# Moving S5 work and weight splits in a fp32 decoder trunk, and cutting its last product into 384 and 128 positions

## The chip, the cores and the metric

The kernel runs on one core of a Trainium2 chip. The metric is the device time of one execution in microseconds. The core has TensorE (PE in the profile: matmuls; PEld: its weight loads), VectorE (DVE), ScalarE (ACT), GpSimd (POOL), SyncE (SP), and 16 DMA engines that move data between memory and the core's SBUF. PSUM banks (`ps`) take the results of matmuls.

## The reference

Two decoder layers on 512 positions of width 1024, in fp32. Each has a mixer (an S5 diagonal state space model beside retention), attention to a memory, and a SwiGLU FFN of inner width 2816, all with RMS norms ahead and residual sums behind; a last RMS norm ends it.

```
for l in range(DEPTH):                       # 2
    proj = rms_norm(x, norm_mix[l]) @ w_in[l]
    u, q, k, v, g = split(proj)
    y_ssm = rms_norm(s5_mixer(u, ...), s5_out_norm[l])
    y_ret = retention(q, k, v, g, ...)
    x = x + concatenate([y_ssm, y_ret]) @ w_out[l]
    x = x + memory_cross_attention(rms_norm(x, ...), ...)
    h = rms_norm(x, norm_ffn[l])
    x = x + (silu(h @ w_gate[l]) * (h @ w_up[l])) @ w_down[l]
return rms_norm(x, norm_final)
```

## The kernel before

Activations lie transposed, 128 features on the partitions and the 512 positions along a row: `xs[0..7]` are eight tiles `x` of 128x512.

**Products.** A fp32 product is made of three fp32r matmuls (`mm3`): high part by high part, high by low, low by high. Activations are split in two tiles (`u_acth` and `u_actl` in the FFN: ACT writes the high part, DVE the difference), and so is each weight chunk of 128x1024.

**Weights.** `prep_chunk` (line 479) brings a chunk: SP issues the load of `raw`, ACT copies it to the high part `w`, and DVE subtracts, `w<-raw,w`, for the low part. For some chunks of layer 0 (`ADDED`) the low part is made without DVE: ACT writes minus the rounded raw tile into it, and POOL issues a DMA that adds the chunk from memory to it. This is called an adding load below; it reads the chunk a second time. There are five `raw` slots.

**FFN** (line 1524). The 22 blocks of 128 inner features go in four parts per layer, 0-6, 6-12, 12-18, 18-22 (`FPARTS`, line 32). In each part the products of gate and up run first, in pairs with 256-column matmuls whose results DVE and ACT merge in `u_gs` and `u_us`; these end in the activations `acts`. Then the part's down product runs: for each of eight output tiles m, six (or four) blocks of `mm3` on 512 positions, and DVE adds the result to `xs[m]`. In the last part of layer 0 the next norm is fed from each finished `xs[m]`.

**S5 work for layer 1.** The tables and matrices of layer 1's S5, in four chunks c of work, are built while layer 0's FFN runs (`s5_load`, `s5_spill`, lines 966 and 1100): DVE, ACT and POOL build, TensorE multiplies, and POOL issues DMAs to scratch memory `sp`; layer 1 fetches it later. `extra["work"]` (line 1742) says after which (first block of the part, m) a half of a chunk is taken up; each chunk has two entries.

**The last part of layer 1** is `last_down` (line 1595), which ends the program: the down product in two halves of 256 positions each; for each half eight `mm3` groups, the sum with `xs` (`u_ly`), its square (`u_lq`), sums of squares over features by TensorE with 1-column matmuls, the inverse root, its spread over the partitions by `spread`, then the output `u_fin` = `u_ly` by gain (`u_lp`) by inverse root. The first half's four outputs are made by POOL, the second's by DVE; SP sends each out.

**Order.** All engine calls are recorded as operations and a list scheduler sets the order on every engine: `due` (line 264) gives each operation a due time from TensorE's program order and the durations of a price table, and `schedule` (line 286) picks for each free engine the earliest due operation whose inputs are ready and whose slots are free. So all instructions have one line in the profile, L410.

Of the kernel before, what the change touches and what calls it, by code (L numbers as in the profile page):

```python
# [18 lines left out]
P = 128  # L19
# [13 lines left out]
HALF = SEQ // 2  # L33

# [388 lines left out]
def trunk(ctx, tc, io):  # L423
# [53 lines left out]
    held = []  # L477

    def prep_chunk(i):
        finish()  # L480
        raw = prog.buf("raw")
        Q.dma_start(out=raw, in_=io["w"][place[i]])
        hi, lo = prog.buf("w"), prog.buf("w")
        S.activation(out=hi, in_=raw, func=AF.Copy)
        if order[i][0] in ADDED and order[i][1] == 0 and (i % 2 == 0 or i > FEW):

            S.activation(out=lo, in_=raw, func=AF.Copy, scale=-1.0)
            G.dma_start(out=lo, in_=io["w"][place[i]].bitcast(F32R), accum_op=add)
        else:
            V.tensor_tensor(out=lo, in0=raw, in1=hi.bitcast(F32), op=sub)  # L490
        ready[i] = (hi, lo)
# [1032 lines left out]
    def ffn(l, nrm, nxt, extra):  # L1524
# [25 lines left out]
        for fa, fb in FPARTS[l]:  # L1550
            acts = []
# [6 lines left out]
            for f in range(fa, fb, 2):  # L1558
                gs = [gen("gs"), gen("gs")]
                us = [gen("us"), gen("us")]  # L1560

                def gated(f=f, gs=gs):
                    if f == 0:
                        nrm.root(True)
                    for g in gs:
                        V.tensor_tensor(out=g, in0=g, in1=nrm.bc, op=mul)
                        S.activation(out=g, in_=g, func=AF.Silu)
                        V.tensor_tensor(out=g, in0=g, in1=nrm.bc, op=mul)

                def merged(f=f, gs=gs, us=us):  # L1570
                    for g, u in zip(gs, us):
                        V.tensor_tensor(out=u, in0=u, in1=g, op=mul)
                    acts.extend(split(u, "act") for u in us)
                gens.append(chain("gate", f, *gs, gated))
                gens.append(chain("up", f, *us, merged))
            run_pairs(gens)
            if nxt is None and fb == NFF:
                last_down(l, fa, acts)
                return
# [15 lines left out]
    def last_down(l, fa, acts):  # L1595
# [3 lines left out]
        for half in range(2):  # L1599
            sl = slice(half * HALF, (half + 1) * HALF)  # L1600
            prog.cap = CAP if half else 2000
            acc, last, ys, ps_ = None, [], [], []

            def gains(m):
                ps_.append(gen("lp"))
                for a in range(2):
                    k = V_FIN + m - 1 + a
                    S.activation(out=ps_[-1][:, a * HALF:(a + 1) * HALF], in_=ys[m - 1 + a],
                                 func=AF.Copy, scale=vec[:, k:k + 1])

            for m in range(KT):
                ps = bank("dn")
                for f in range(n):
                    blk = m * n + f
                    b = (blk % 8) * P
                    mm3(ps[:, :HALF], cut(ws[blk // 8], slice(None), slice(b, b + P)),
                        cut(acts[f], slice(None), sl), f == 0, f == n - 1)
                y, sq = gen("ly")[:, :HALF], gen("lq")[:, :HALF]
                V.tensor_tensor(out=y, in0=ps[:, :HALF], in1=xs[m][:, sl], op=add)
                S.activation(out=sq, in_=y, func=AF.Square)  # L1620
                ys.append(y)
                if m % 2 == 1 and m < KT - 1:
                    gains(m)
                if m >= KT - 2:
                    last.append(sq)
                elif acc is None:
                    acc = sq
                else:
                    new = gen("la")[:, :HALF]
                    V.tensor_tensor(out=new, in0=acc, in1=sq, op=add)  # L1630
                    acc = new
            cols = [bank("lc")[:, :1] for _ in range(2)]
            for x in [acc] + last:
                for j in range(2):
# [3 lines left out]
            m, y, t = small("lm", 2), small("ly", 2), small("lt", 2)  # L1638
            for j in range(2):
# [8 lines left out]
            spread(pb, y, 2)  # L1648
            bc = pb[:, :HALF]
            if half == 0:  # L1650

                bc = gen("lbc")[:, :HALF]
                S.activation(out=bc, in_=pb[:, :HALF], func=AF.Copy)
            eng = G if half == 0 else V
            for i in range(KT // 2):
                y, o = ps_[i], gen("fin")
                pair = lambda x: x.rearrange("p (a t) -> p a t", a=2)
                eng.tensor_tensor(out=pair(o), in0=pair(y), op=mul,
                                  in1=bc.unsqueeze(1).to_broadcast([P, 2, HALF]))
                Q.dma_start(out=prog.perm(dest[2 * i * P:(2 * i + 2) * P, sl].rearrange(  # L1660
                    "(a p) t -> p a t", a=2)), in_=pair(o))
# [60 lines left out]
    for l in range(L):  # L1722
# [6 lines left out]
        if l + 1 < L:  # L1729
            def work(c):  # L1730
                if c == 0:
                    extra["ld"] = s5_load(l + 1)
                if c not in half:
# [3 lines left out]
            extra["work"] = {(0, 0): 0, (0, 2): 0, (6, 0): 1, (6, 2): 1, (12, 0): 2, (12, 2): 2,  # L1737
                             (12, 4): 3, (12, 6): 3}
# [103 lines left out]
```

## Time and profile before

| | us |
|---|---|
| time, median of 3 runs | 1464.76 (1464.25 to 1468.72) |
| the profiled execution | 1465.04 |
| its span | 1463.2 |
| PE busy | 1448.3 (99%) |
| DVE busy | 1185.9 (81%) |
| ACT busy | 799.3 (55%) |
| POOL busy | 101.2 (7%) |
| FFN of layer 0, parts one to three | 97.92, 95.52, 97.44 |
| FFN of layer 1, first and third part | 93.65, 92.83 |
| last down of layer 1 on PE | 24.40 |
| from there to the span's end | 10.84 |

The span is the profiled execution from first to last instruction, and the device time has 1.84 us around it. The stages are stretches of the span, cut where TensorE goes from one part's work to the next. Busy time is of the instructions that are not register, branch, semaphore or DMA-issuing ones.

### The profile page before, as it was taken

The page shows a single profiled execution, that of the slowest core. Times are in us where ns is not written, and L with a number is a line of the kernel's source. Part 1 is how long each engine was busy: PE and PEld are TensorE (multiplying, and loading weights), DVE is VectorE, ACT ScalarE, POOL GpSimd, SP SyncE. Part 2 cuts the span into 40 slices and gives each one's busy share as a digit, 9 for nine tenths or more (in the row PEclk, how much of TensorE's full clock was granted, in tenths as well). Part 3 has the DMA queues.
Part 4 walks back from the last instruction along what each step waited for, and adds up shares of the span by engine and source line. Part 5 has one row for each costly group of instructions (what it writes and reads, how often), then busy time and mean ns, then how long its engine had stood idle before and what let it go on. Part 6 is the DMA issues. An engine that isn't in the chain of part 4 may idle for free.

```text
span 1463.2 us, 23062 instructions
## 1 busy us (share of the span) xinstructions
PE 1448.3 (99%) x8784; PEld 1274.3 (87%) x8784; DVE 1185.9 (81%) x2073; ACT 799.3 (55%) x1381; POOL 101.2 (7%) x207
## 2 busy tenths in 40 slices
PE   8999999999999999999999999999999999999997
PEld 7887888888898998988988888888889989999897
DVE  8889996666999896997964989757679969869595
ACT  6798665444665463565635346644456625436264
POOL 5721000000001001002000000000000000000001
PEclk9999999999999999999999999999999999999998
DMA  8556443212135233244445444332112323413221
GB/s 286 149 121 184 158 143 128 90 58 73 58 105 177 90 131 125 98 143 155 144 139 192 141 157 137 127 133 89 62 58 73 125 77 102 144 59 125 91 87 58
DMA packets 68175, 175.35 MB, mean 120 GB/s; under 512 B 11360, under 2 KB 23008, under 8 KB 68064
## 3 DMA queue, kind: packets, MB, share of 16 engines
q1 hardware_dynamic: 64240, 160.77, 33.0%
q0 software_dynamic: 3824, 13.11, 3.5%
q8 instruction: 69, 1.13, 0.3%
q14 instruction: 42, 0.34, 0.1%
HBM read 159.43 MB, written 13.63 MB: 118 GB/s over the span
## 4 chain that ended last, share of the span: by engine, by line
PE 91%; DVE 5%; DMA 2%; ACT 1%; issue 1%; SPq 0%; DVEq 0%; ACTq 0%
PE ps L410 91%; DVE w L410 1%; DVE u_gs L410 1%; DVE u_us L410 1%; ACT w L410 1%; DMA u_angq<-in_pos_dram 0%; DMA raw<-in_w_dram 0%; DVE raw L410 0%; DMA x<-in_xT_dram 0%; DMA u_w<-in_w_dram 0%; DVE u_mt L410 0%; SPq L410 0%; DVE u_actl L410 0%; DVE u_la L410 0%; ACT u_lq L410 0%
## 5 line engine op out<-in xcount | busy, mean ns | idle before, releaser
L410 ACT ACTIVATE w<-raw 128x1024 fp32r<-128x1024 f32 x353 | 352.9, 1005 | 423.0 <-PE ps L410 347.0
L410 PE MATMUL ps<-u_nff,w 128*128 128x256 f32 x3696 | 439.2, 280 | 0.6 <-DVE w L410 0.4
L410 PEld LDWEIGHTS ps<-u_nff,w 128*128 128x128 f32 x3696 | 436.2, 188 | 4.1 <-DVE w L410 1.4
L410 DVE TENSOR_TENSOR w<-raw,w 128x1024 fp32r<-128x1024 f32 x331 | 378.8, 1151 | 51.1 <-ACT w L410 50.5
L410 PE MATMUL ps<-u_acth,w 128*128 128x512 f32 (+1 forms) x768 | 224.5, 375 | 0.3 <-ACT u_acth L410 0.3
L410 PEld LDWEIGHTS ps<-u_acth,w 128*128 128x128 f32 x768 | 139.7, 188 | 26.3 <-ACT u_acth L410 0.7
L410 PE MATMUL ps<-u_nmh,w 128*128 128x512 f32 x480 | 157.0, 398 | 0.5 <-DVE w L410 0.5
L410 PE MATMUL ps<-u_actl,w 128*128 128x512 f32 (+1 forms) x384 | 143.9, 377 | 1.4 <-DVE u_actl L410 1.2
L410 DVE TENSOR_TENSOR x<-ps,x 128x512 f32<-128x512 f32 x88 | 60.5, 689 | 99.1 <-PE ps L410 99.0
L410 PEld LDWEIGHTS ps<-u_nmh,w 128*128 128x128 f32 x480 | 89.7, 188 | 19.0 <-DVE w L410 0.9
L410 PE MATMUL ps<-u_nml,w 128*128 128x512 f32 x240 | 95.1, 396 | 0.0
L410 PEld LDWEIGHTS ps<-u_actl,w 128*128 128x128 f32 x384 | 72.2, 188 | 16.9 <-DVE u_actl L410 3.7
L410 PE MATMUL ps<-u_nch,w 128*128 128x512 f32 x256 | 81.7, 393 | 0.0
L410 PE MATMUL ps<-u_xoh,w 128*128 128x512 f32 x256 | 80.7, 392 | 0.0
L410 DVE TENSOR_TENSOR raw<-raw 128x512 f32<-128x512 f32 x88 | 60.3, 685 | 6.1 <-DMA raw<-in_ws_dram 5.9
L410 DVE TENSOR_TENSOR raw<-raw,raw 128x512 f32<-128x512 f32 x88 | 60.3, 685 | 0.3
L410 DVE TENSOR_TENSOR u_gs<-u_gs,u_nfry 128x512 f32<-128x512 f32 x88 | 59.5, 689 | 0.3
L410 POOL TENSOR_TENSOR u_fin<-u_lp,u_lbc 128x512 f32<-128x512 f32 x4 | 5.4, 1393 | 767.4 <-ACT u_lbc L410 767.4
L410 PEld LDWEIGHTS ps<-u_nch,w 128*128 128x128 f32 x256 | 48.1, 188 | 10.4
L410 PEld LDWEIGHTS ps<-u_xoh,w 128*128 128x128 f32 x256 | 48.0, 188 | 9.9
L410 PEld LDWEIGHTS ps<-u_nml,w 128*128 128x128 f32 x240 | 45.2, 188 | 9.1 <-issue 0.2
L410 PE MATMUL ps<-u_xol,w 128*128 128x512 f32 x128 | 50.3, 393 | 0.0
(369 smaller groups left out, 2463.7 us busy)
## 6 DMA issues: line engine op xcount, KB each, us to landing
raw<-in_w_dram SPq DMA_DIRECT2D x166, 512.0 KB, 3.6
raw<-in_ws_dram SPq DMA_DIRECT2D x88, 512.0 KB, 3.7
u_s5x<-sp SPq DMA_DIRECT2D x28, 256.0 KB, 4.1
w<-in_w_dram POOLq DMA_DIRECT2D x11, 512.0 KB, 5.4
u_mr<-in_memT_dram SPq DMA_DIRECT2D x12, 256.0 KB, 3.9
x<-in_xT_dram SPq DMA_DIRECT2D x8, 256.0 KB, 4.4
tu<-u_u SPq DMA_DIRECT2D x8, 256.0 KB, 3.5
u_ub<-tu SPq DMA_DIRECT2D x32, 64.0 KB, 3.5
```

The lines of the kernel that those rows point to most:

```text
L410: getattr(engines[o.eng], o.fn)(**k)
```

## The change

Three edits, which go together.

1. In layer 0's FFN the half-chunks of S5 work for layer 1 are taken up after m = 2 and m = 4 of each part's down, chunk c in part c. Before it was m = 0 and 2 for chunks 0 to 2, and m = 4 and 6 of the third part for chunk 3, which is now in the last part.
2. The down chunks 0, 2, 4 and 6, 8, 10 of layer 0's first two parts are made with adding loads: for each of six chunks, one DVE subtraction less, one ACT copy and one POOL DMA more.
3. `last_down` cuts the positions 384 and 128 instead of 256 and 256. The first piece has the `mm3` products on 384 columns; the second has one fp32 matmul in place of three products, with the raw weight (kept in `raws`) by the unsplit activation (`whole`). The first piece's outputs are eight of 128x384 each, six on POOL and two on DVE (`rest`); the second's are two of 128x512 (four row blocks of 128 positions).

```
-        if order[i][0] in ADDED and order[i][1] == 0 and (i % 2 == 0 or i > FEW):
-            S.activation(out=lo, in_=raw, func=AF.Copy, scale=-1.0)
-            G.dma_start(out=lo, in_=io["w"][place[i]].bitcast(F32R), accum_op=add)
+        if added(i):
+            add_load(lo, raw, io["w"][place[i]])

+    def added(i):
+        x = order[i]
+        if x[1] > 0:
+            return False
+        if x[0] in ADDED:
+            return i % 2 == 0 or i > FEW
+        a, b = FPARTS[0][:2]
+        if x[0] == "down":
+            return x[2] < b[1] and x[2] % 2 == 0
+        return False

+        for first in (True, False):
+            sl = slice(0, QUART) if first else slice(QUART, SEQ)
...
+                    if first:
+                        mm3(ps[:, :w], cut(ws[blk // 8], slice(None), b),
+                            cut(acts[f], slice(None), sl), f == 0, f == n - 1)
+                    else:
+                        T.matmul(out=ps[:, :w], lhsT=raws[fa + blk // 8][:, b],
+                                 rhs=whole[f][:, sl], start=f == 0, stop=f == n - 1)
...
+            for i in range(KT // per):
+                if not first:
+                    scaled(V, i)
+                elif i < KT - 2:
+                    scaled(G, i)
+                else:
+                    rest.append(lambda i=i, f=scaled: f(V, i))

-            extra["work"] = {(0, 0): 0, (0, 2): 0, (6, 0): 1, (6, 2): 1, (12, 0): 2, (12, 2): 2,
-                             (12, 4): 3, (12, 6): 3}
+            extra["work"] = {(a, m): c for c, (a, b) in enumerate(FPARTS[l]) for m in (2, 4)}
```

Where the order of instructions moves, it moves as follows. First DVE in layer 0's first part, where gate and up end and the down begins; `u_mt`, `u_mb`, `u_s5bb` are S5 rows, `u_us`, `u_actl` the FFN's. Before:

```order
L410 TENSOR_TENSOR u_us<-u_us,u_gs 128x512
L410 TENSOR_TENSOR u_mt_4667<-u_s5bb,rr_165 128x256
L410 TENSOR_TENSOR u_mb<-u_mt_4648 128x256
L410 TENSOR_TENSOR u_us<-u_us,u_gs 128x512
L410 TENSOR_TENSOR u_mb<-u_mt_4667 128x256
L410 TENSOR_TENSOR u_mt_4697<-u_s5c,pr_161 128x256
L410 TENSOR_TENSOR u_mt_4700<-u_s5c,pi_162 128x256
L410 TENSOR_TENSOR u_actl<-u_us,u_acth 128x512
L410 TENSOR_TENSOR u_mt_4697<-u_s5c,pi_162 128x256
L410 TENSOR_TENSOR u_mt_4700<-u_s5c,pr_161 128x256
L410 TENSOR_TENSOR w_110<-raw_105,w_111 128x1024
L410 TENSOR_TENSOR w_114<-raw_106,w_115 128x1024
```

The same place on DVE now:

```order
L411 TENSOR_TENSOR u_us<-u_us,u_gs 128x512
L411 TENSOR_TENSOR u_gs<-u_gs,u_nfry 128x512 x2
L411 TENSOR_TENSOR u_actl<-u_us,u_acth 128x512
L411 TENSOR_TENSOR u_us<-ps_118,u_us 128x256
L411 SCALAR_TENSOR_TENSOR u_us<-ps_122,u_us 128x512
L411 TENSOR_TENSOR u_actl<-u_us,u_acth 128x512
L411 TENSOR_TENSOR u_gs<-u_gs,u_nfry 128x512
L411 TENSOR_TENSOR u_us<-u_us,u_gs 128x512 x2
L411 TENSOR_TENSOR w_114<-raw_106,w_115 128x1024
L411 TENSOR_TENSOR u_actl<-u_us,u_acth 128x512 x2
L411 TENSOR_TENSOR u_s5bb<-u_s5b,fr_163 128x256
L411 TENSOR_TENSOR u_s5bt<-u_s5b,fi_164 128x256
```

All `u_actl` now stand ahead of the S5 rows, and one of the weight splits `w<-raw,w` is gone from between them.

Then POOL's queue in the first part, with the memsets and copies of the S5 work. Before:

```order
L410 COPY u_ckr<-u_s5c 128x4x16
L410 TENSOR_SCALAR u_cki<-u_s5c 128x4x16
L410 TENSOR_TENSOR u_diag<-s5d_139,eye_12_140 32x256
L408 MEMSET u_dt 128x512
L408 MEMSET u_car 128x512
L408 MEMSET u_cai 128x512
L410 DMA sp_181<-u_btr 128x512
```

And now:

```order
L411 COPY u_ckr<-u_s5c 128x4x16
L411 TENSOR_SCALAR u_cki<-u_s5c 128x4x16
L411 DMA w_112<-in_w_dram 128x1024
L411 TENSOR_TENSOR u_diag<-s5d_139,eye_12_140 32x256
L411 DMA w_110<-in_w_dram 128x1024
L409 MEMSET u_dt 128x512
L411 DMA w_112<-in_w_dram 128x1024
L409 MEMSET u_car 128x512
```

The three adding loads of the first part's down chunks now stand between the S5 preparation and its memsets.

Last, TensorE at the program's end; `c,u_lq` and `c,u_la` are the sums of squares, `ident,s` the spread. Before:

```order
L410 MATMUL ps_118<-u_acth,w_112 128x256
L410 MATMUL ps_118<-u_actl,w_112 128x256
L410 MATMUL ps_118<-u_acth,w_113 128x256
L410 MATMUL ps_116<-c_150,u_la 128x1
L410 MATMUL ps_116<-c_150,u_lq 128x1
L410 MATMUL ps_123<-c_150,u_la 128x1
L410 MATMUL ps_123<-c_150,u_lq 128x1
L410 MATMUL ps_116<-c_150,u_lq 128x1
L410 MATMUL ps_123<-c_150,u_lq 128x1
L410 MATMUL ps_120<-ident_141,s_101 128x128 x2
```

And now:

```order
L411 MATMUL ps_123<-u_us,raw_103 128x128 x2
L411 MATMUL ps_121<-ident_141,s_67 128x128 x3
L411 MATMUL ps_123<-u_us,raw_103 128x128 x2
L411 MATMUL ps_116<-u_us,raw_104 128x128 x4
L411 MATMUL ps_117<-u_us,raw_104 128x128 x4
L411 MATMUL ps_119<-u_us,raw_105 128x128 x4
L411 MATMUL ps_120<-u_us,raw_105 128x128 x4
L411 MATMUL ps_118<-c_150,u_la 128x1
L411 MATMUL ps_118<-c_150,u_lq 128x1 x2
L411 MATMUL ps_122<-ident_141,s_101 128x128
```

The second piece's products have 128 columns and raw weights; three sums and one spread follow them where it were six and two, and the first piece's spread of three stands among them.

## Rows read from the trace of the kernel before

**Rows 1.** The chain that ended last, shares of the span by engine:

```profile
PE 91%; DVE 5%; DMA 2%; ACT 1%; issue 1%; SPq 0%; DVEq 0%; ACTq 0%
```

**Rows 2.** Stages: us, busy of PE PEld DVE ACT POOL (instructions), clock, DMA share, GB/s:

```profile
387.83:485.75 97.92, 96.00 (x676) 87.60 (x675) 93.64 (x160) 55.94 (x95) 10.70 (x19) 1.00 0.38 128
485.75:581.27 95.52, 95.43 (x674) 88.07 (x673) 81.56 (x130) 50.37 (x83) 7.06 (x15) 1.00 0.36 120
581.27:678.71 97.44, 97.35 (x697) 89.47 (x696) 89.33 (x156) 57.99 (x99) 12.46 (x24) 1.00 0.38 126
678.71:718.35 39.64, 39.64 (x337) 39.63 (x336) 36.39 (x51) 23.69 (x38) 0.00 (x0) 1.00 0.41 143
718.35:740.30 21.95, 21.95 (x98) 17.95 (x97) 20.41 (x30) 13.92 (x20) 0.00 (x0) 1.00 0.39 133
1108.69:1202.34 93.65, 93.52 (x652) 86.41 (x650) 81.74 (x122) 48.80 (x78) 0.00 (x0) 1.00 0.30 102
1295.50:1388.33 92.83, 92.83 (x650) 86.53 (x649) 74.44 (x104) 43.04 (x66) 0.00 (x0) 1.00 0.30 103
1427.96:1452.36 24.40, 24.40 (x210) 24.40 (x209) 16.03 (x38) 15.24 (x36) 5.44 (x4) 1.00 0.13 44
1452.36:1463.20 10.84, 2.81 (x18) 2.35 (x16) 3.87 (x11) 1.97 (x6) 0.00 (x0) 0.63 0.30 98
```

**Rows 3.** Timeline of PE where two parts' downs begin: start, duration, instruction, [idle before]:

```profile
450.55 0.97 PE L410 MATMUL ps<-u_acth,w 128*128 128x512 f32 x3 [0.26 <-ACT u_acth L410]
...
457.55 0.85 PE L410 MATMUL ps<-u_acth,w 128*128 128x512 f32 x3
459.62 0.50 PE L410 MATMUL ps<-u_actl,w 128*128 128x512 f32 x1 [1.22 <-DVE u_actl L410]
...
548.81 0.40 PE L410 MATMUL ps<-u_acth,w 128*128 128x512 f32 x1
549.30 0.51 PE L410 MATMUL ps<-u_actl,w 128*128 128x512 f32 x1
```

**Rows 4.** Timeline of DVE ahead of the first wait, same columns:

```profile
458.55 0.41 DVE L410 TENSOR_TENSOR u_mt<-u_s5c,pi 128x256 f32<-128x256 f32 x1
458.88 0.68 DVE L410 TENSOR_TENSOR u_actl<-u_us,u_acth 128x512 fp32r<-128x512 f32 x1
...
460.15 2.35 DVE L410 TENSOR_TENSOR w<-raw,w 128x1024 fp32r<-128x1024 f32 x2
```

**Rows 5.** Landing of POOL's adding loads; DMA issues of 52 to 62 us, last the median landing:

```profile
DMA to landing us min/median/max: 5.1/5.4/8.8
...
raw<-in_w_dram SPq DMA_DIRECT2D x2, 512.0 KB, 4.7
w<-in_w_dram POOLq DMA_DIRECT2D x1, 512.0 KB, 8.8
```

**Rows 6.** Timeline of PE at fp32 matmuls of 128 columns, two records each:

```profile
79.73 1.06 PE L410 MATMUL ps<-u_ub,u_btr 128*128 128x128 f32 x8
80.54 0.71 PE L410 MATMUL ps<-u_nmh,w 128*128 128x512 f32 x2
```

**Rows 7.** Timeline of the program's end; the POOL row is the first half's:

```profile
1444.87 5.44 POOL L410 TENSOR_TENSOR u_fin<-u_lp,u_lbc 128x512 f32<-128x512 f32 x4 [767.42 <-ACT u_lbc L410]
...
1452.56 0.42 DVE L410 TENSOR_TENSOR u_ly<-ps,x 128x256 f32<-128x256 f32 x1 [0.33 <-PE ps L410]
...
1454.11 0.48 ACT L410 ACTIVATE s<-ps,c 128x1 f32<-128x1 f32 x2 [0.27 <-DVE s L410]
...
1456.69 2.48 DVE L410 TENSOR_TENSOR u_fin<-u_lp,ps 128x512 f32<-128x512 f32 x4 [1.31 <-PE ps L410]
```

**Rows 8.** DMA packets of 1458.3 to 1461.4 us, then 162.5 to 163, and its queue:

```profile
DMA packets 1073, 1.04 MB, mean 336 GB/s; under 512 B 55, under 2 KB 1073, under 8 KB 1073
...
DMA packets 206, 0.09 MB, mean 187 GB/s; under 512 B 31, under 2 KB 205, under 8 KB 206
q1 hardware_dynamic: 206, 0.09, 64.3%
```

## What the change should do to the time

> **What bounds the kernel now.** I read the chain of work that ended last first: TensorE holds 91% of it [rows 1]. A change can therefore gain only where TensorE stands still, where it is given less work, or behind its last matmul. Next I read the busy time by stage. The two layers have the same weight work in their FFN, so the parts can be set side by side: the first takes 97.92 us in layer 0 and 93.65 in layer 1, the third 97.44 and 92.83 [rows 2]. Layer 0 builds the S5 chunks of layer 1 there, one in the first part and two in the third. TensorE's busy time is more by 2.48 and by 4.52; half of the latter, 2.26, is about what a chunk's own matmuls cost, and moving a chunk keeps that. So of the first part's 4.27 us of difference 2.0 are not matmuls. The span minus busy time there, 1.92, is TensorE standing still; in the two later parts it is 0.09 each [rows 2]. To it come waits which the busy time hides, since a matmul that waits inside is counted long; I find them where each part's down begins. In part 0 a run of three products starts at 457.55, and at 0.23 each it would be over at 458.24; the next, which needs `u_actl`, starts at 459.62, so 1.39 us are lost, and a row at 450.55 stood idle for 0.26 [rows 3]. Parts 1 and 2 show a wait of 0.26 each: a row at 548.81 is followed only at 549.30, and a like pair stands 95 us later [rows 3]. Together 1.39 + 0.26 + 0.52 = 2.17 us; the stretches allow 2.0 in the first part and with the later waits about 2.6.
>
> DVE's own rows tell why part 0 loses most. DVE is 93.64 of 97.92 us busy in it [rows 2], and between the last product of gate and up and the `u_actl` that TensorE wants it does five S5 operations of 0.42 us, one of which is the row at 458.55; the wanted row begins at 458.88, and two weight splits of 1.15 us follow it before the next `u_actl` [rows 4].
>
> **S5 work two blocks further on.** In the new order all `u_actl` stand ahead of that part's S5 rows. The five rows ahead of the wanted one, 5 x 0.34 = 1.7 us at their spacing, no longer stand there, and the weight split that now stands ahead of the last one is wanted anyway. I take off the 1.39, the 0.26 (its releaser is ACT, which writes `u_acth` [rows 3]; I count it in full, as ACT waits for DVE's `u_us`) and 0.35 of the 0.52 in the later parts: -2.0 us. Layer 1 speaks for nearly all of it: the same products without S5 rows on DVE have a span 0.13 over TensorE's busy time in the first part and equal to it in the third [rows 2]. The bounds are 0, where ACT or the splits become last in the same place, and -2.6, all that the stretches show. The S5 matmuls themselves cost the same later.
>
> Chunk 3 moves to the last part (18 to 22) of the same FFN, where DVE was 20.41 of 21.95 us busy during the down [rows 2]. There its rows stand between those of the next norm. The order leaves 19 matmuls of about 0.23 us, 4.3 us, between the last of these norm rows and its first use, and the cover is that. I take 0, up to +0.5 if some norm row comes late. That part's TensorE time grows by the chunk's 2.2 us, and part 2 loses as much.
>
> **Six adding loads.** Six splits of 1.17 us (2.35 for two [rows 4]) go from DVE, 7.0 us in all, which is room on an engine that TensorE waits for only in the places above. ACT gets six copies; it is 55.94 of 97.92 us busy in the worst part [rows 2]. POOL issues six accumulating DMAs of 512 KB: the memory reads these chunks twice. The price is the landing: 5.1 to 8.8 us from issue, 5.4 in the middle, over the 11 there are; the 8.8 is a single load in a stretch where two `raw` loads run beside it and have 4.7 themselves [rows 5]. In the new order I counted TensorE's work between each issue and the first matmul that reads the added tile, at 0.118 us for 256 columns (39.64 us by 336, the same in both layers) and 0.229 for 512 (21.95 by 96) [rows 2]: 6.9 us for the first chunk of part 0, 6.0 for that of part 1, and 10.5 to 17.1 for the other four. So only the first of each part is near. Both are flanked by SP's `raw` loads of the next chunks. At 5.4 both are hidden, at 8.8 they cost 1.9 + 2.8 = 4.7 us. TensorE can fill with products of other blocks, which the counts contain. I take a landing of 6.5 us with a little over, +1.0 us; ends 0 and +4.7.
>
> The Trainium skill (DMA: Bandwidth & Descriptors, "Issuing engines are not separate DMA queues") says that transfers issued by SP, ACT and POOL share the same 16 engines and interleave. By it a load issued on POOL gets no path of its own, and the long landing of 8.8 is the rule wherever raw loads run; rival C is what it would give.
>
> **The last down part, 384 and 128 positions.** TensorE's stretch is now 24.40 us: 192 products of 256 columns at 0.118 (22.66) and 16 records for the sums and spreads, 1.74, or 0.109 each [rows 2]. New: 96 products of 384 columns. Three quarters of the 512-column price give 0.1715, one and a half times the 256-column price 0.177; I take 0.1733, 16.64 us. Then 32 fp32 matmuls of 128 columns. Their nearest rows are S5's: eight records, two to a matmul, from 79.73 to the next start at 80.54, so 0.20 to 0.224 each [rows 6]; at the upper value 7.14 us. The sums need 24 records instead of 16, 2.6 us. Together 26.4, +2.0 us (ends +1.2 and +2.4). It is a loss on the path, since TensorE was full here.
>
> What follows TensorE's last product gets shorter, because the second piece has half the columns [rows 7]. The last `u_ly`, 0.42 us on 256 columns, drops by about 0.13, and the square behind it by 0.1; the sums over two column groups become one, -0.22; the two square roots, 0.48, become one, -0.24; the spread of four records becomes two, -0.22 by the same 0.109 each; four output products on DVE, 2.48, become two, -1.2. Together -2.1 (ends -1.2, where transfers set the end and not DVE, and -2.3). POOL and DVE finish the first piece meanwhile: four POOL products took 5.44 [rows 7], six of 384 columns take about 6 to 7. Today the first half's products end near 1427.96 + 96 x 0.118 = 1439.3 and POOL begins 5.6 us later; the first piece ends near 1444.6, so POOL would begin near 1450.2 and end near 1456.5; the last DVE products would begin near 1458. That cover is 1.5 us.
>
> The final outputs are half the bytes but in packets of 512 B instead of 1024 B. Today the end is filled with transfers: 1.04 MB at 336 GB/s [rows 8], 3.1 us. The same price for half of it is 1.56. In a stretch of almost only 512-B packets 187 GB/s came at 64.3% busy [rows 8], so 290 GB/s at full, 1.8 us; by equal time to a packet it would be 3.1. I take +0.3 for it and for the one 384-column output that lies among them (-0.3 to +1.7). Net for the last part: +2.0 - 2.1 + 0.3 = +0.2 us, ends -1.1 and +2.9.
>
> The Trainium skill (DMA: Bandwidth & Descriptors, "Why small descriptors are slow (HBM only)") gives a fixed overhead of some three cycles to each packet, 19 against 35 beats for 512 and 1024 B. An estimate by that is 1.7 us for the two last outputs, between my ends; no row here has such a transfer alone.
>
> **Sum.** -2.0 + 1.0 + 0 + 0.2 = -0.8 us. The profiled execution has 1465.04 us, a span of 1463.2 and 1.84 around it, so 1464.24 is its counterpart; it lies 0.28 over the median 1464.76, so I say 1464.0.
>
> **Rivals.**
> A, the forecast: the stall goes, and the two other parts nearly cancel. 1464.0, spread 1462.4 to 1465.6.
> B: the adding loads land under 6 us and the end is shorter by its full tail, -2.0 + 0 - 1.1 = -3.1, up to -3.7 with all 2.6 of stalls: 1461.1 to 1461.7. For it: the median landing is 5.4 [rows 5]. Against it: the longest is of the one stretch shown in which raw loads run beside it.
> C, slower: the first adding load of a part lands late. Place: the first down chunk of parts 0 and 1; price: TensorE waits landing minus 6.9 and minus 6.0; at 8.8 that is 4.7, so -2.0 + 4.7 + 0.2 = +2.9 and 1467.7. It decides the sign when the two landings reach about 7.4 us, where the waits (0.5 + 1.4) equal what the S5 move gains less the last part's 0.2. For it: raw loads run on both sides. Against it: half of the 11 loads landed in 5.4 or less [rows 5].
> D: the last part loses. The small packets cost as much as large ones, and the first piece's outputs on POOL hold SP's queue beyond 1458: +2.9 instead of +0.2, with the rest as forecast 1466.7.
> E: the S5 move only shifts the wait, to the ACT copy or the weight splits; no 2.0, so 1466.0.
>
> **How the numbers follow.** A 0.53, B 0.15, C 0.17, D 0.08, E 0.07. The range, 1461.2 to 1467.4, reaches from the outer half of B to most of C and leaves out little else. A measurement of this kernel tells about 0.3% from no change, 4.4 us. For faster by that it must be under 1460.4: a tail of B with stalls that the rows hide, 0.06. For slower, above 1469.2: C at more than 8.8 on both loads, or C with D, 0.06. The rest, 0.88, is the same.
>
> **What would show it.** Right: after the first gate and up of layer 0 no TensorE wait for `u_actl` over 0.3 us; part 0's stretch near 96.6 where it is 97.92 now (-1.8 for the stalls, +0.5 for the load); part 2 near 95.0, as its second chunk is gone, and the last part's down near 24; TensorE's last-part stretch near 26.4; from its end to the span's end 9.0 instead of 10.84. Wrong: a TensorE wait for a tile `w` that a DMA wrote, in the first down of part 0 or 1, POOL landings above 7.4 there, a last-part stretch beyond 26.8, or the last output's issue waiting for POOL.

## The result, and the profile after

The changed kernel is slower: 1473.84 us in the median of 6 runs (1470.76 to 1476.25), against 1465.62 of the kernel before in 6 runs. The ratio is 1.0054 with a 95% interval of 1.0042 to 1.0065, about 7.9 us. The profiled execution took 1473.45 us with a span of 1471.7. The forecast was 1464.0 with a range up to 1467.4, so it missed the size and the sign.

TensorE still holds the chain that ended last, with 90% where it was 91% [rows 1], and what it waits for has changed. In the view of TensorE's waits the columns are who waited, for whom, us in total, times, and the longest:

```profile
PE ps L411 <- DMA w<-in_w_dram: 4.8, 2, 3.3
PE ps L411 <- DVE u_la L411: 2.3, 1, 2.3
```

Neither row exists in the kernel before: the first are the adding loads, the second is a sum of squares in the last part. The stages of after, with the columns of [rows 2], are the three first parts of layer 0's FFN, the last part's down, and the last down of layer 1 up to its last product and from there to the span's end:

```profile
388.21:485.67 97.46, 95.86 (x676) 88.13 (x674) 90.08 (x157) 58.32 (x98) 25.61 (x21) 1.00 0.46 145
485.67:585.70 100.03, 96.46 (x674) 88.96 (x672) 78.80 (x127) 52.91 (x86) 9.86 (x18) 0.98 0.42 130
585.70:680.67 94.97, 94.66 (x673) 87.50 (x672) 81.76 (x130) 50.55 (x83) 9.52 (x19) 1.00 0.35 121
720.27:744.97 24.70, 24.70 (x123) 19.64 (x121) 24.19 (x47) 18.34 (x31) 3.85 (x7) 1.00 0.53 186
1433.14:1459.80 26.66, 26.66 (x186) 26.36 (x184) 17.63 (x38) 15.32 (x34) 3.41 (x3) 1.00 0.02 8
1459.80:1471.70 11.90, 2.46 (x8) 2.00 (x8) 4.67 (x13) 2.13 (x8) 3.14 (x4) 0.58 0.48 160
```

Beside [rows 2], part 0 is 0.46 us shorter, part 1 is 4.51 longer, part 2 is 2.47 shorter and the last part's down 2.75 longer, since chunk 3 went from the one to the other. The last down and what follows take 38.56 us instead of 24.40 + 10.84 = 35.24, so 3.32 more. These places sum to 7.65 of the 8.5 us by which the span grew.

The largest piece is at the first adding load of part 1. TensorE's timeline there (start, duration, instruction, idle before it):

```profile
546.39 0.40 PE L411 MATMUL ps<-u_acth,w 128*128 128x512 f32 x1
550.06 0.94 PE L411 MATMUL ps<-u_acth,w 128*128 128x512 f32 x2 [3.27 <-DMA w<-in_w_dram]
550.79 0.63 PE L411 MATMUL ps<-u_actl,w 128*128 128x512 f32 x1
551.22 1.05 PE L411 MATMUL ps<-u_acth,w 128*128 128x512 f32 x2
552.07 0.63 PE L411 MATMUL ps<-u_actl,w 128*128 128x512 f32 x1
552.50 1.05 PE L411 MATMUL ps<-u_acth,w 128*128 128x512 f32 x2
553.35 0.62 PE L411 MATMUL ps<-u_actl,w 128*128 128x512 f32 x1
553.78 0.42 PE L411 MATMUL ps<-u_acth,w 128*128 128x512 f32 x1
```

The matmul at 550.06 waited 3.27 us. Behind it three products take 1.16 to 1.28 us instead of 0.69. The busy-time view of that stretch says why, in the last but two column, the granted clock:

```profile
550.00:553.80 3.80, 3.74 (x10) 2.93 (x11) 1.46 (x5) 0.00 (x0) 0.00 (x0) 0.55 1.03 275
```

The clock is 0.55 for 3.8 us after TensorE stood idle for 3.27, near the lower of its levels of 1.2 and 2.4 GHz. So the wait cost about another 1.7 us: the nine products from 550.06 to 553.78 took 3.72, and at 0.229 apiece they would have taken 2.06. In part 0 the same kind of wait was 1.55 us, and the products behind it ran at full pace.

What the adding load did in this time is in the chain of the stretch from 540 to 552 (start, length, what):

```profile
540.91 9.11 DMA w<-in_w_dram
550.02 0.04 issue
550.06 2.22 PE ps L411 x5
```

It landed 9.1 us after its issue. Over the 17 adding loads the landing is now 5.0 to 9.1 with 7.1 in the middle [rows 5]:

```profile
DMA to landing us min/median/max: 5.0/7.1/9.1
```

### The profile page after: what moved, and what is told of

Its sections match the earlier page's. It is cut to its first block, busy times and chain, and to the rows that moved or that the text cites. A ratio compares the mean times of both kernels' runs of the same rounds, so it can differ in the third digit from the quotient of the medians.

```text
span 1471.7 us, 23011 instructions
## 1 busy us (share of the span) xinstructions
PE 1451.4 (99%) x8752; PEld 1276.4 (87%) x8752; DVE 1180.6 (80%) x2067; ACT 804.0 (55%) x1387; POOL 120.3 (8%) x215
## 4 chain that ended last, share of the span: by engine, by line
PE 90%; DVE 5%; DMA 2%; ACT 1%; issue 1%; SPq 0%; DVEq 0%; ACTq 0%
PE ps L411 90%; DVE w L411 2%; DMA w<-in_w_dram 1%; DVE raw L411 1%; DVE u_gs L411 1%; ACT w L411 1%; SPq L411 0%; DMA u_angq<-in_pos_dram 0%; DMA raw<-in_w_dram 0%; DVE u_us L411 0%; DMA x<-in_xT_dram 0%; DVE u_fin L411 0%; DVE u_la L411 0%; DVE u_actl L411 0%; DVE u_nma L411 0%
## 5 line engine op out<-in xcount | busy, mean ns | idle before, releaser
L411 ACT ACTIVATE w<-raw 128x1024 fp32r<-128x1024 f32 (+1 forms) x359 | 358.5, 1005 | 429.2 <-PE ps L411 337.6
L411 DVE TENSOR_TENSOR w<-raw,w 128x1024 fp32r<-128x1024 f32 (+1 forms) x325 | 370.8, 1147 | 53.2 <-ACT w L411 49.3
L411 PE MATMUL ps<-u_acth,w 128*128 128x512 f32 (+1 forms) x704 | 218.1, 389 | 4.8 <-DMA w<-in_w_dram 4.8
L411 PEld LDWEIGHTS ps<-u_acth,w 128*128 128x128 f32 x704 | 132.2, 189 | 31.9 <-DMA w<-in_w_dram 5.7
L411 PE MATMUL ps<-u_actl,w 128*128 128x512 f32 (+1 forms) x352 | 137.0, 391 | 0.0
L411 PEld LDWEIGHTS ps<-u_actl,w 128*128 128x128 f32 x352 | 66.5, 189 | 14.2 <-DVE u_actl L411 1.3
L411 POOL TENSOR_TENSOR u_fin<-u_lp,u_lbc 128x384 f32<-128x384 f32 x6 | 6.5, 1124 | 714.0 <-ACT u_lbc L411 714.0
```

What stands on the lines that cost most here:

```text
L411: getattr(engines[o.eng], o.fn)(**k)
```

## The experiments

All times below stand against runs of the kernel before on the same chip, in ratios whose 95% interval is about 0.09% to either side, 1.3 us (some 0.18% for the two kernels that hold raw loads back, which have four runs each); "us from before" is the ratio's difference by 1465.

**One part alone, or taken back.** Four kernels divide the change. Without the new adding loads:

```
-        if x[0] == "down":
-            return x[2] < b[1] and x[2] % 2 == 0
```

> The changed kernel with the six down chunks split by DVE again (no new adding loads); S5 move and 384/128 cut stay. Theory L (late landing): in the changed kernel TensorE stands 1.55 us in part 0 and 3.27 us in part 1 for the added low tile, and behind the second wait runs 3.7 us at half clock, 1.8 us more; without the loads 6.6 us of the 8.4 us loss are gone: about 1467 us, no wait for a DMA-written w, part 1 near 95.3 us instead of 100.03. Rival S (the S5 chunk in the last part crowds DVE, the loads only fill idle time): 1471 or more, and the waits turn into waits for DVE's w or u_actl in the same places. Rival E (the program's end costs it all): 1473.

With the last down part as before (the function `last_down` of the kernel before put in the place of the new one):

> The changed kernel with the last down part cut 256/256 as before; S5 move and all adding loads stay. Theory L: only the 3.3 us that the end grew by (38.56 us against 35.24 from the start of the last down part) come off: about 1470.5 us, part 1 still near 100. Rival E: 1465 to 1466. If the end loses nothing by itself (it is shifted noise): 1473.

The S5 move alone, on the kernel before (line 1737 there):

```
-            extra["work"] = {(0, 0): 0, (0, 2): 0, ...}
+            extra["work"] = {(a, m): c for c, (a, b) in enumerate(FPARTS[l]) for m in (2, 4)}
```

> The kernel before with the S5 work taken up after m = 2 and 4 of each part and nothing else. Theory L and the forecast's first term: the 1.39 us and smaller waits for u_actl go, 1.5 to 2.2 us faster than before: about 1463.5. Rival S: 2 us or more slower, with waits in the last part's down or at the start of layer 1's mixer.

The S5 move, the old last part, and adding loads for four chunks:

```
+            return x[2] < b[1] and x[2] % 2 == 0 and x[2] % 6 != 0
```

> S5 move, 256/256 as before, adding loads only for down chunks 2, 4, 8, 10, so not for the first chunk of a part. Theory L: those four have 10 us or more from issue to first use and landed in 7.5 to 9.0 us, so no wait for them; as fast as the S5 move alone within 0.7 us, about 1463.5. Rival S: 1468 or more. If a load's traffic itself slows others: 1465 to 1467, with raw loads landing later.

| kernel | median us | ratio to before (95%) | us from before |
|---|---|---|---|
| all of the change | 1473.84 | 1.0054 (1.0042 to 1.0065) | +7.9 |
| without new adding loads | 1467.08 | 1.0003 (0.9994 to 1.0012) | +0.4 |
| old last part | 1470.24 | 1.0020 (1.0010 to 1.0030) | +2.9 |
| S5 move alone | 1463.93 | 0.9985 (0.9976 to 0.9994) | -2.2 |
| S5 move, four late adding loads | 1464.03 | 0.9984 (0.9976 to 0.9993) | -2.3 |

All four medians of the parts came within 0.6 us of what theory L put down; the rivals S (the S5 chunk crowds DVE) and E (the end costs all) are out. By the ratios the adding loads cost 5.1 us over the S5 move alone, the new last part 2.6, and the four late adding loads nothing. The three parts sum to 5.5 of the 7.9 us; the medians give 6.3, 3.2 and in sum 7.4 of 8.2. The rest, 2.4 or 0.8 us, is within what these intervals add up to.

The first two parts of layer 0's FFN in the S5 move alone, with the columns of [rows 2]; the first of them shows the forecast's first term at its place:

```profile
390.31:486.43 96.12, 96.06 (x675) 88.43 (x674) 93.44 (x160) 56.35 (x95) 21.84 (x17) 1.00 0.39 130
486.43:581.66 95.23, 94.77 (x673) 87.32 (x672) 81.88 (x130) 50.53 (x83) 7.37 (x15) 1.00 0.37 121
```

97.92 became 96.12, and span and busy time differ by 0.06 instead of 1.92.

**Are the first chunks alone to blame?** The complement of the last kernel has adding loads only for chunks 0 and 6 (`x[2] % 6 == 0`), with the old last part.

> S5 move, 256/256 as before, and adding loads only for the first down chunk of parts 0 and 1 (chunks 0 and 6). Theory L: these two carry all that the adding loads cost, since their raw loads and the next chunks' are queued right ahead of them: within 1.5 us of the 1470.2 of all six loads, and 5 to 7 us over the S5 move alone. If the traffic of six loads together makes them late: 1464 to 1467, with landings of 5 to 6.5 us for these two.

It took 1468.77 us, ratio 1.0025 (1.0016 to 1.0034): 5.9 us over the S5 move alone by the ratios, 4.8 by the medians. The two first chunks carry the whole cost. Their waits were 3.5 us together, and they landed in 7.9 and 7.8 us though no other of the six ran, so it is not the number of adding loads that makes them late. The same two parts in this kernel:

```profile
388.36:486.03 97.67, 96.06 (x676) 88.13 (x674) 92.41 (x159) 56.81 (x96) 24.60 (x19) 1.00 0.42 134
486.03:583.23 97.20, 94.89 (x674) 87.82 (x673) 80.96 (x129) 51.45 (x84) 8.05 (x16) 1.00 0.38 123
```

They are 1.55 and 1.97 us longer than in the S5 move alone, 3.5 together, which is the waits and nothing more, at a granted clock of 1.00. Much of the rest of the 4.8 to 5.9 goes with the mean granted clock of the whole run: the three runs of this kernel that have 0.998 took 1466.2 to 1467.8 us, the seven with 0.996 or 0.997 took 1468.3 to 1471.2, and the S5 move alone has 0.997 or 0.998 in all of its eleven. That the clock fell behind these waits in the seven, as it did in the changed kernel's trace, is likely from that, but no trace of them shows it.

**What makes the landing late?** Two causes were named, raw loads in the same transfer engines, or POOL and DVE. First, in the kernel with all adding loads and the old last part, the raw loads of the gate and up weights of parts 1 and 2 were cut to 16 of 1024 columns:

```
-        Q.dma_start(out=a, in_=io["ws"][i, 0])
-        Q.dma_start(out=b, in_=io["ws"][i, 1])
+        n = 16 if order[at][1:3] in ((0, 6), (0, 12)) else 2 * h
+        for x, r in ((a, 0), (b, 1)):
+            Q.dma_start(out=x[:, :n], in_=io["ws"][i, r][:, :n])
```

> As the run with all adding loads and 256/256, but the raw loads of the gate and up weights of parts 1 and 2 bring 16 of 1024 columns, so that nearly no traffic runs beside the adding loads; those weights are then stale and the sums wrong. The order is unchanged. Theory T (the landing grows from 5.4 to 7.1 us and more since raw loads share the transfer engines): landings of 5.1 to 6 us, no wait for the added tile, and 1470.2 falls to about 1464. Rival G (POOL's own start is late, its descriptors held up by busy DVE and POOL work): the first packet still starts 2.4 to 3.7 us behind the issue, landings of 6.5 to 8 us, waits of 0.5 to 2.5 us, 1466 to 1469.

1468.55 us, ratio 1.0021 (1.0012 to 1.0029), and waits of 2.8 us: theory T's time was missed, and the number is what rival G had put down. The landings tell why. The raw loads cut were not those ahead of the two tight loads: there SP issues raw loads of down chunks, which were left whole. For the third adding load of part 1, whose only neighbours were cut, the DMA issues read, first in the changed kernel from 558 to 568 us and then here from 556 to 566 (KB each, us to landing):

```profile
w<-in_w_dram POOLq DMA_DIRECT2D x1, 512.0 KB, 8.2
```

```profile
w<-in_w_dram POOLq DMA_DIRECT2D x1, 512.0 KB, 5.2
raw<-in_ws_dram SPq DMA_DIRECT2D x2, 8.0 KB, 1.6
```

With the neighbour gone the landing is 5.2; in the kernel from which this one was made, with the neighbour whole, it is 6.8. The waits that stayed belong to the loads that kept theirs.

Then the adding load by itself, in a kernel that does nothing else:

```
    for raw, dve, pw in ((0, 0, 0), (1, 0, 0), (0, 1, 0), (1, 1, 0), (0, 0, 1), (1, 1, 1), ...):
        start()                      # ACT writes lo and what the others wait for
        G.dma_start(out=lo, in_=io["w"][8].bitcast(F32R), accum_op=add)
        ...                          # four raw loads, eight subtractions, three products on POOL
```

> A kernel of its own, which computes nothing of the reference: one adding load of 512 KB in six settings, each twice: alone, beside four raw loads, beside eight DVE subtractions of 128x1024, beside both, with three POOL products of 128x256 behind it, and with all. Then four POOL products of 128x384 alone, twelve DVE additions of 128x128 alone, and both together. Theory T: alone 5.1 to 5.4 us, beside raw loads 7 to 9, beside DVE alone no more than 5.5. Rival G: beside DVE alone 6.5 or more, beside raw loads alone under 6.5. Theory P: DVE's additions take 0.29 us alone and about 0.9 beside POOL's products; otherwise 0.29 in both.

Two of its stretches, the issues of the load beside eight DVE subtractions and then beside raw loads (three of the four issues are in the stretch):

```profile
lo<-in_w_dram POOLq DMA_DIRECT2D x1, 512.0 KB, 5.5
```

```profile
raw<-in_w_dram SPq DMA_DIRECT2D x3, 512.0 KB, 7.4
lo<-in_w_dram POOLq DMA_DIRECT2D x1, 512.0 KB, 10.0
```

DVE at work changes nothing: 5.5 us, as theory T had it, and POOL's products behind the issue change nothing either. Four raw loads make it 9.1 to 10.1 in all six stretches that have them, more than the 7 to 9 that theory T put down. Rival G is out.

Whether raw loads take bandwidth or a place in the queue is told by issuing them ahead of the adding load or behind it:

> A kernel of its own, which computes nothing of the reference: one adding load with 0, 1, 2 or 4 raw loads of 512 KB issued by SP about 1 us ahead of it, and with 2 or 4 issued about 1 us behind it; each setting twice. Theory F (the adding load waits for what was queued ahead): its first packet starts 1.6 us from issue with none ahead, about 1.5 us later for each raw load ahead beyond the first, 4.7 with four; with loads behind it the first packet stays at 1.6 and the landing under 6.5. Theory B (they only share the bandwidth): landings of 7 us or more with four behind as well as with four ahead.

The start of the load's first packet (from the times of the packets in the trace) and the end of its last, two of each setting:

```
raw loads         first packet, us from issue   last packet's end, us from issue
none              1.7, 1.6                      5.1, 5.0
1 ahead           1.6, 1.6                      4.9, 5.1
2 ahead           2.5, 2.5                      6.1, 6.8
4 ahead           4.6, 4.6                      8.8, 9.3
2 just behind     1.6, 1.6                      6.0, 6.0
4 just behind     1.6, 1.6                      5.9, 5.7
```

Theory F holds in this kernel: four loads issued 0.8 us behind it or later cost the adding load 0.8 us, the same four issued up to 1.5 us ahead cost it some 4 us, 3.0 of them in waiting for its first packet. In the changed kernel SP issues two raw loads within 1.2 us ahead of each tight adding load, and the adding loads' first packets start 3.9 and 2.5 us from issue. The number of loads ahead does not say it all. The two stood 1.5 and 1.1 us ahead here, and 0.7 and 0.2 us ahead in part 0, so more of them was left; and the tight loads landed in 7.9 and 9.1 us, where two ahead end at 6.1 to 6.8 here. Other raw loads follow behind them in the changed kernel; their share was not measured apart.

Two kernels tried to use that: with adding loads only for chunks 0 and 6, SP's raw loads of the next two down chunks were made to wait for a column that ACT writes behind the negated copy, and then for some 1.7 us more.

```
+        if order[i][0] == "down" and order[i][1] == 0 and order[i][2] < 12 and order[i][2] % 6 in (1, 2):
+            S.activation(out=raw[:, :1], in_=token[0], func=AF.Copy)
```

> As the run with only the two first adding loads (1468.8 us, waits of 3.5 us, first packets 2.9 and 3.6 us from issue), but SP's raw loads of the two next down chunks wait for a column that ACT writes behind the negated copy, so that the adding load is issued ahead of them. Theory F (first come, first served in the transfer engines): first packet 1.6 us from issue, landing 5.0 to 6.2 us, no wait over 0.7 us for it, 1463.5 to 1465.5 us unless the held raw loads are late themselves. Rival G (POOL's issue is slow in this place whatever is queued): first packets stay at 2.9 us or more and the time at 1467 to 1470. If the held loads make the next splits late: waits for w written by DVE of 1 us or more there, 1466 to 1468.

> As the run in which SP's raw loads were held by one ACT copy, but held about 1.7 us longer (three more copies of 512 columns on ACT ahead of the column that SP waits for). Theory F (what is in the transfer engines' queue first goes first): the adding load's first packet starts 1.5 to 2.2 us from issue instead of 4.7 to 5.0, it lands within 6.5 us, and the waits for the added tile fall from 8.1 us together to under 1.5; since the raw loads and ACT's copies are late by design, waits for DVE's w or for u_acth may come instead, 1465 to 1472 us. Rival G (POOL's issue itself is slow here): first packets at 2.9 us or more, waits of 3 us and more.

Both were slower, 1478.48 (ratio 1.0095, 1.0079 to 1.0112) and 1474.73 us (1.0069, 1.0049 to 1.0088), and the expected first packets at 1.6 did not come: they came at 5.0 and 4.7 us in the first and at 3.6 and 2.6 in the second. The hold had bunched the raw loads: in the first, SP issued three at 444.09 to 444.97 and POOL its load at 445.00. In the second, two were issued at 444.15 and 444.58, ahead of POOL's 445.06. So neither kernel got the load to the front; what they add is the count: two loads ahead gave 2.6 and 3.6, three gave 4.7 and 5.0. That the order of issue can be mended inside the kernel was not shown.

**The end.** In the kernel without new adding loads POOL's six output products of the first piece were cut to 8 of 384 columns:

```
-                eng.tensor_tensor(out=wide(o), in0=wide(ps_[i]), op=mul,
-                                  in1=bc.unsqueeze(1).to_broadcast([P, per, w]))
+                n = w if eng is V else 8
+                eng.tensor_tensor(out=wide(o)[:, :, :n], in0=wide(ps_[i])[:, :, :n], op=mul, ...)
```

> As the run without new adding loads (S5 move and 384/128 cut), but the six products of the first piece's output on POOL work on 8 of 384 columns, in place, and the six outputs go out mostly unscaled; the order is unchanged. Theory P (POOL's products slow DVE's sums beside them, 0.9 us instead of 0.29 each, and so hold up TensorE's last sums by 2.3 us): DVE's u_la go back to 0.29 us, the 2.3 us wait falls under 0.7, and the time comes to about 1464.3 from 1467.1. Rival W (the end is longer since TensorE has 2 us more work there): 1466.5 or more.

The median fell from 1467.08 to 1464.09, as theory P had it; by the ratios (1.0003 to 0.9996) the drop is 1.0 us with some 1.9 to either side, which alone would decide nothing. The traces decide. DVE at the end, first in the changed kernel, then without POOL's products:

```profile
1456.47 2.61 DVE L411 TENSOR_TENSOR u_fin<-u_lp,u_lbc 128x384 f32<-128x384 f32 x2
1459.00 0.28 DVE L411 TENSOR_TENSOR u_ly<-ps,x 128x128 f32<-128x128 f32 x1
1459.20 0.88 DVE L411 TENSOR_TENSOR u_la<-u_la,u_lq 128x128 f32<-128x128 f32 x1
...
1460.21 1.88 DVE L411 TENSOR_TENSOR u_la<-u_la,u_lq 128x128 f32<-128x128 f32 x2
...
1462.14 0.59 PE L411 MATMUL ps<-c,u_la 128*128 128x1 f32 x2 [2.34 <-DVE u_la L411]
```

```profile
1449.48 1.02 DVE L411 TENSOR_TENSOR u_fin<-u_lp,u_lbc 128x384 f32<-128x384 f32 x2
1450.42 0.28 DVE L411 TENSOR_TENSOR u_ly<-ps,x 128x128 f32<-128x128 f32 x1
1450.62 0.28 DVE L411 TENSOR_TENSOR u_la<-u_la,u_lq 128x128 f32<-128x128 f32 x1
```

With POOL at work the two products on DVE take 2.61 us instead of 1.02, and each sum `u_la` 0.9 instead of 0.28, while `u_ly`, which reads one operand from PSUM, stays at 0.28. The 2.34 us wait of TensorE is gone without POOL's products, and the stretch from the first product of the last part to the span's end is 35.8 us (1426.13 to 1461.9), where the run without new adding loads had 38.2. The kernel made for this alone has the same rows, twelve DVE additions of 128x128 alone and then beside four POOL products:

```profile
170.91 2.51 DVE L79 TENSOR_TENSOR pr<-y,big 128x128 f32<-128x128 f32 x12 [11.68 <-ACT big L46]
...
175.59 5.71 DVE L79 TENSOR_TENSOR pr<-y,big 128x128 f32<-128x128 f32 x12 [2.17 <-ACT big L46]
175.81 4.74 POOL L75 TENSOR_TENSOR mem<-y,big 128x384 f32<-128x384 f32 x4 [7.57 <-ACT raw L49]
```

DVE takes 3.2 us more, POOL 0.5 more than its 4.21 alone. This is what the Trainium skill states (SBUF — State Buffer, "SBUF: two separate sides"): GpSimd and a DVE operation with two SBUF operands share a port pair that one holds for a whole instruction. The rows agree: beside POOL's products it is the additions with both operands in SBUF that grow, and `u_ly`, which has one in PSUM, does not.

All eight products on POOL instead of six (`elif i < KT:`), again without new adding loads:

> As the run without new adding loads, but all eight output products of the first piece are on POOL, none on DVE. Theory P: POOL is busy for two products more, some 8.7 us, DVE's sums stay slow beside it, and the wait of TensorE stays or shrinks only by the 2.6 us that the two DVE products held DVE's queue, less what the sums lose: 1465.5 to 1467, and POOL ends near the last DVE products. Rival Q (only DVE's two products, 2.6 us in front of the second piece's sums, hold up the end): 1464.5. If POOL's later end sets the end: over 1468.

1467.91 us, ratio 1.0017 (1.0008 to 1.0026): no gain, so rival Q is out. It is 0.9 us above the range that theory P put down. DVE's sums came through in 0.4 to 0.6 us now, but POOL worked longer, and DVE's last steps of the root, 128x1 each, met it:

```profile
1455.25 0.53 DVE L411 TENSOR_TENSOR s<-s 128x1 f32<-128x1 f32 x1
1455.81 1.87 DVE L411 SCALAR_TENSOR_TENSOR s<-s,s 128x1 f32<-128x1 f32 x2
...
1457.73 0.49 PE L411 MATMUL ps<-ident,s 128*128 128x128 f32 x2 [3.20 <-DVE s L411]
```

Two operations that take 0.35 us elsewhere took 1.87, and TensorE's wait moved from the sums to the spread, 3.2 us.

**Chunk 3.** The S5 move with chunk 3 kept in the third part:

```
+            extra["work"] = {(a, m): c for c, (a, b) in enumerate(FPARTS[l][:3]) for m in (1, 3)}
+            extra["work"].update({(12, 5): 3, (12, 7): 3})
```

> The S5 move on the kernel before, but chunk 3 stays in the third part (halves of the chunks after m = 1 and 3, chunk 3 after m = 5 and 7). The forecast's second term (chunk 3 in the last part costs nothing): equal to the S5 move alone, 1463.9, within 0.7 us. If the last part pays for it: 0.7 to 2 us faster than that, 1462 to 1463. If two chunks in one part crowd DVE there: 1464.7 or more, with a wait in part 2 or at the start of the last part.

1463.52 us, ratio 0.9988 (0.9979 to 0.9997), against 1463.93 and 0.9985: the same. Where chunk 3 stands is worth nothing that these runs can tell.

The fastest kernels here are the S5 move alone and its two variants (0.9984 to 0.9988, each with an interval that ends below 1). They beat both kernels of the case.

## Why the prediction was wrong, step by step

**The S5 move: right.** -2.0 us was forecast, -2.2 measured, and the place was right: the wait for `u_actl` in part 0 is gone. Chunk 3 in the last part was priced at 0 and costs 0.

**The adding loads: the step that failed.** The mechanism was rival C's, and it was on record with the right place, the first chunk of parts 0 and 1. Its signs of being wrong came true, a wait for a `w` that a DMA wrote and landings above 7.4. The term was mis-sized: +1.0 was taken from ends of 0 and 4.7, and it cost 5 to 6. Two things went into that. First, the choice of 6.5 us for the landing leaned to the middle of eleven loads, nine of which have no raw load issued in the 2 us ahead, and not to the row with raw loads beside it, 8.8 [rows 5]. That row was the nearest: the forecast had itself found that SP's raw loads stand on both sides. Nor is it the only long one. The trace of before has a second, from 131 to 142 us, with SP's loads of `raw` and of the memory tiles `u_mr` around it, which the forecast did not count:

```profile
u_mr<-in_memT_dram SPq DMA_DIRECT2D x4, 256.0 KB, 7.5
raw<-in_w_dram SPq DMA_DIRECT2D x2, 512.0 KB, 9.0
w<-in_w_dram POOLq DMA_DIRECT2D x1, 512.0 KB, 7.9
```

The loads landed in 7.9 and 9.1 us, and with the 6.9 and 6.0 us of TensorE's work that the forecast had counted, this gives 1.0 and 3.1; the waits were 1.55 and 3.27. The counting was good to half a microsecond. Second, the upper end had no term for the clock behind a wait: 1.7 us at a granted clock of 0.55 in the profiled execution. Both landings were above the forecast's own break-even, 7.4 us, so rival C, which had a chance of 0.17, named what happened; its price of +2.9 in all was still too low, by the clock and by the last part.

**The last part: wrong in one step of four.** TensorE's products were priced at +2.0 and came to 26.66 against 24.40, +2.26, inside the stated ends. An fp32 matmul of 128 columns cost what was taken, 0.223 us: 36 records stand in 4.18 us in the changed kernel and 35 in 4.07 in the run without POOL's products, so 0.11 a record, two to a matmul. The tail without disturbance came out as forecast: from the last product to the end 9.1 us in the run without POOL's products, and 9.04 (10.84 - 2.1 + 0.3) forecast. What failed is "POOL and DVE finish the first piece meanwhile": a cover of 1.5 us was worked out from POOL's end alone, as if DVE ran beside it at its own speed. With POOL's products it is 11.9. Rival D had the right place and the wrong way: POOL's products hold up DVE's sums, not SP's queue. The profile of before shows it, in rows that the forecast did not read, DVE beside POOL's 5.44 us [rows 7] and just behind it:

```profile
1446.40 1.30 DVE L410 TENSOR_TENSOR u_la<-u_la,u_lq 128x256 f32<-128x256 f32 x1 [0.48 <-ACT u_lq L410]
1448.52 0.63 DVE L410 TENSOR_TENSOR u_la<-u_la,u_lq 128x256 f32<-128x256 f32 x1 [0.48 <-ACT u_lq L410]
1451.47 0.42 DVE L410 TENSOR_TENSOR u_la<-u_la,u_lq 128x256 f32<-128x256 f32 x1 [0.55 <-ACT u_lq L410]
```

One shape has 1.30, 0.63 and 0.42 us; there it hid, since TensorE had a half of the positions still to do.

Even with that gone the cut gains nothing: without POOL's products, and so with less work, the kernel took 1464.09 us, and the S5 move with even halves 1463.93; in their traces the last part from its first product to the span's end is 35.8 and 34.7 us.

**What stays open.** The rest of the span's growth lies between the FFNs: layer 1's FFN began 5.67 us late where the last part of layer 0 had ended with 4.60. Most of the 1.07 us between is a stretch of some 50 us, up to 1002 us, in which TensorE's products came every 233 ns instead of 229. Eight of the thirteen whole-kernel traces have 233 there and five 229; the kernel before and the two made from it alone are among the five, with two that were made from the changed one. What sets it was not found. Open too is what part of the adding loads' cost is the clock's in the runs that were not traced.

## What to carry to other kernels

A transfer that is issued late and needed soon is priced by what the queue ahead of it holds, so list the loads issued in the 1.5 us before it and take the landing of a row with the same neighbours, not a median over the program. Give the upper end of a wait on TensorE a term for a lower clock behind it, here 1.7 us, and do not count on it either way. Before a stretch's operations are shortened or moved beside POOL, look whether one DVE shape has several durations in the trace: where it has, the two engines are in each other's way, and POOL's work is not free cover.

## What the runs showed of the hardware

- In a kernel that does nothing else, an adding load of 512 KB starts its first packet 1.6 to 1.7 us from issue and lands in 5.1 to 5.6 us; DVE's or POOL's work beside it changes neither. Two and four raw loads of 512 KB ahead move the first packet to 2.5 and 4.6 us. The same loads just behind do not, and the load then ends at 5.7 to 6.0.
- After an idle time of 3.27 us TensorE ran at a granted clock of 0.55 for 3.8 us; after 1.55 us idle it did not slow. The length of the wait alone does not decide it. In the S5 move alone the clock fell soon after a wait of 1.26 us, and with adding loads for chunks 0 and 6 it stayed up behind one of 2.00 us (each wait, then the stretch behind it):

```profile
32.63 1.05 PE L410 MATMUL ps<-c,u_nma 128*128 128x1 f32 x8 [1.26 <-DVE u_nma L410]
34.20:37.60 3.40, 3.40 (x10) 2.61 (x9) 3.40 (x11) 0.00 (x0) 3.24 (x5) 0.51 0.84 247
...
549.17 0.73 PE L411 MATMUL ps<-u_acth,w 128*128 128x512 f32 x2 [2.00 <-DMA w<-in_w_dram]
549.17:553.00 3.83, 3.83 (x17) 3.17 (x18) 2.69 (x6) 0.07 (x1) 0.00 (x0) 1.00 0.83 288
```

- Products of 512 columns start every 229 ns in most stretches and every 233 in some, at a granted clock of 1.00 in both; a stretch of some 50 us, near 950 to 1000 us, had the one in the kernel before and the other in the changed one, about 0.9 us apart.
- POOL's own operations stretch as well beside a busy DVE: four products of 128x384 took 4.74 us instead of 4.21 beside twelve DVE additions. A product of 32x256 took 4.84 us in part 0 of the changed kernel, where two of the same form in before had a mean of 0.66; DVE was busy there too, but that DVE was the cause is not shown.
